# Moving the decode states and the W_out sums to other units, and one more pair of output rows as seven products

## The chip, the cores and the metric

The kernel runs on one core of a Trainium2 chip. The metric is device time in microseconds (us) of one execution of the whole program. Before the change three runs took 1107.13, 1110.31 and 1109.86 us, a median of 1109.86 us. One more execution was recorded by the profiler; it took 1107.08 us, and all views of the trace are views of it. TensorE (PE in the profile) does the matmuls, VectorE (DVE) and ScalarE (ACT) the elementwise work, GpSimd (POOL) small statistics; DMAs are issued by SyncE (SP), by ACT and by POOL, each with an in-order queue of its own.

## The reference

One layer of a hybrid decoder on 2048 prompt tokens and, beside them, one new token for each of 8 sequences ("decode"). Cut to what matters:

```python
h = rmsnorm(x, norm_g)
rq, rk, rv, rg, hq, hf, hi, hgate = split(h @ w_in, 8)          # 8 groups of 512 columns
o_ret, s_ret = recurrence(rotary(rq), rotary(rk) * dk**-0.5, rv, log_gamma, s_ret)   # 4 heads of 128
o_hg,  s_hg  = recurrence(silu(hq), (1 - lb) * sigmoid(-hf), hi, logf, s_hg)         # 4 heads of 128
o_cat = concat(head_rmsnorm(o_ret) * silu(rg), head_rmsnorm(o_hg) * silu(hgate))
y = rmsnorm(x + o_cat @ w_out, final_norm_g)
# recurrence: S_t = diag(f_t) S_{t-1} + k_t v_t^T ; o_t = S_t^T q_t
```

For the prompt the state starts at zero and the recurrence is computed in chunks. For the decode tokens it is one step from a given state: eight heads (four of retention, four of HGRN2), each with 8 states of 128x128. Outputs are y for both, and all new states. Every float32 operand is split into a high and a low part, and a product is three matmuls (high by high, high by low, low by high).

## The kernel before, in words

**Stages.** First the values (rv and hi) of all 2048 tokens are computed and put in DRAM (lines pv and pvd of the profile). Then come 16 *units*, numbered 0 to 15, two for each head and half of the sequence (`order`). Even units project an HGRN2 head, odd units a retention head. A unit's projection is three weight blocks of 128 columns (`sub_steps`, `seg_steps`, matmuls at L557). While a unit projects, the scan of the unit before it is merged in between its steps (`merge`): so an even unit carries a **retention** scan (`ret_rec`) and an odd unit an **HGRN2** scan (`hgrn_rec`), which has many more VectorE operations. Units 0 to 7 are the first half of the tokens, 8 to 15 the second. Units 0, 7, 8 and 15 run segment by segment with all three weights live (`SEG_MAJOR`). Scan results go to DRAM (`o_dram`).

**Side work.** `side_at` lists operations with a place, unit number plus fraction; `side_steps` and `place` put them among the projection steps. Before the change these are, all in units 8 to 15:

- the eight decode heads. `d_load` loads the 8 states S (512 KB) and the values, broadcast over partitions, vb (512 KB) on SP's queue. `d_state` multiplies vb by k (L937), for HGRN2 also S by f (L940); `d_add` adds them (L946, L948), copies the high part (ACT, L950) and writes the new state out on ACT's queue; `d_lo` makes the low part (L958); `d_mm` is two matmuls for each of two halves (L965), a copy and a write to `d_dram`.
- four `t_spool(k)`. Each loads two blocks of W_out (512 KB each), makes four differences of them (L906 to L909), splits two 128x1024 results into high and low (`split`, L106 and L107) and writes four parts of 512 KB to `t_dram` on ACT's queue. They are the sums T1 to T4 of W_out that the seven-product form needs.
- `d_norm`, `d_sq`, `d_ms`, `d_rs`, `d_tr`: reading the eight decode outputs back from `d_dram`, their head norm, and eight transposes on PE.

**Output stage.** 2048 rows are 16 chunks of 128. `PLAIN = 6` chunks are done directly (`out_steps`, 48 matmuls of 128x128x512 each, py in the profile); the first two are merged with the scan of unit 15, and there too lies `d_project`, the output projection of the decode tokens (32 matmuls, pyd). The other ten chunks go in pairs: `o_pair` computes a pair with seven products of four blocks (84 matmuls, po) after sums on the left (`op_s12`, `op_s34`) and with T1 to T4 on the right, read back from `t_dram` by `t_load` on POOL's queue, 1 MB for each high or low part. T4 is put in columns of `wo[0]` that the direct chunks read before.

**Buffers.** `rawp` has six slots of 4 KB a partition, used by loads of weights (wr), states and values (dS, dv), their high and low parts (ds), W_out (wot, wor), outputs (or), y rows and more. `wp` has three slots each for high and low weight parts (w_h, w_l), and `split` takes its results from there too. A slot is free when its last reader is done, a DMA out of it included.

**What sets the order.** PE's instructions run in the order in which the program text emits them. For the other engines and queues a planner orders the instructions beforehand: it walks the program with estimated durations and lets an engine take a later instruction when the earlier ones are not ready in its estimate and a buffer slot is free. On the chip each queue then runs strictly in that order, so an instruction that waits holds all behind it on its queue.

Of the kernel before, what the change touches and what calls it, by code (L numbers as in the profile page):

```python
# [10 lines left out]
F32 = mybir.dt.float32  # L11
F32R = mybir.dt.float32r
# [6 lines left out]
P = 128  # L19
# [22 lines left out]
def step_kernel(ctx, tc, a, out):  # L42
# [66 lines left out]
    def split(r, name):  # L109
        h = wp.tile([P, D], F32R, tag="wh", name=name + "h")  # L110
        l = wp.tile([P, D], F32R, tag="wl", name=name + "l")
        hi_lo(h, l, r)
        return h, l
# [785 lines left out]
        (x, n): dr.tile([P, 2, 4, GW], F32, tag=f"t{x}{n}", name=f"t_dram{x}{n}") for x in "hl" for n in range(2)  # L899
    }  # L900

    def t_spool(k):
        ra, rb, t = (rawp.tile([P, 2, GW], F32, tag="raw", name=f"wot{k}{n}") for n in range(3))
        for n, r in enumerate((ra, rb)):
            sp.dma_start(r.rearrange("p a b -> p (a b)"), a["w_out"][(k + 4 * n) * P : (k + 4 * n + 1) * P, :])
        dve.tensor_tensor(t[:, 1], rb[:, 1], ra[:, 1], op=ALU.subtract)  # L906
        dve.tensor_tensor(ra[:, 1], ra[:, 1], ra[:, 0], op=ALU.subtract)
        dve.tensor_tensor(t[:, 0], rb[:, 1], ra[:, 1], op=ALU.subtract)
        dve.tensor_tensor(ra[:, 0], t[:, 0], rb[:, 0], op=ALU.subtract)  # L909
        for n, src in enumerate((t, ra)):  # L910
            for x, y in zip("hl", split(src.rearrange("p a b -> p (a b)"), f"wos{k}{n}")):
                act.dma_start(t_dram[x, n][:, :, k], y.bitcast(F32).rearrange("p (a b) -> p a b", a=2))

    dec = {}

    def d_split(src, name):
        t = up.tile([P, 8, 40], F32R, tag="dhl", name=name, bufs=2)
        act.activation(t[:, :, 0:8], src, AF.Copy)
        act.activation(t[:, :, 8:32], zero.unsqueeze(1).to_broadcast([P, 8, 24]), AF.Copy)
        dve.tensor_tensor(t[:, :, 32:40], src, t[:, :, 0:8].bitcast(F32), op=ALU.subtract)  # L920
        return t
# [6 lines left out]
        sp.dma_start(vb, vd_dram[ty, :, h * P : (h + 1) * P].partition_broadcast(P))  # L928
        dec["l", hd] = (S, vb)

    def d_state(hd):
        ty, h = divmod(hd, NH)
        if hd == 0:
            dec["q"] = d_split(dq, "dq_hl")
        S, vb = dec["l", hd]
        kd = dk[:, hd].unsqueeze(2).to_broadcast([P, NB, P])
        dve.tensor_tensor(vb, vb, kd, op=ALU.mult)  # L937
        if ty == 1:
            fd = df[:, hd].unsqueeze(2).to_broadcast([P, NB, P])
            dve.tensor_tensor(S, S, fd, op=ALU.mult)  # L940

    def d_add(hd):
        ty, h = divmod(hd, NH)
        S, vb = dec["l", hd]
        if ty == 0:
            dve.scalar_tensor_tensor(S, S, GAMMA[h], vb, op0=ALU.mult, op1=ALU.add)  # L946
        else:
            dve.tensor_tensor(S, S, vb, op=ALU.add)  # L948
        sh, sl = (rawp.tile([P, NB, P], F32R, tag="raw", name=f"ds{t}{hd}") for t in "hl")
        act.activation(sh, S, AF.Copy)  # L950
        act.dma_start(
            out[("new_ret_sample", "new_hgrn_sample")[ty]][0, :, h].rearrange("b d v -> d b v"), S
        )
        dec["s", hd] = (sh, sl)

    def d_lo(hd):
        sh, sl = dec["s", hd]
        dve.tensor_tensor(sl, dec["l", hd][0], sh.bitcast(F32), op=ALU.subtract)  # L958

    def d_mm(hd, part):  # L960
        for i in (part,):
# [44 lines left out]
    def d_project():  # L1006
        ps = [ps_o.tile([40, 512], F32, tag="o", name=f"pyd{i}") for i in range(2)]
        t = rawp.tile([NB, 2, 512], F32, tag="raw", name="ydl")
        for i in range(2):
            m = 0  # L1010
            for k in range(KT):
                for w in wo[k // 4]:
                    pe.matmul(
                        ps[i], dec["od"][:, k], w[:, k % 4, i * 512 : (i + 1) * 512],
                        start=(m == 0), stop=(m == 2 * KT - 1),
                    )
# [280 lines left out]
    def o_pair(i, after):  # L1297
        ca, cb = 2 * i, 2 * i + 1
        last = cb == T // P - 1
        box = {}  # L1300
        lo, hi = slice(0, GW), slice(GW, D)
        ms = {c: sm.tile([P, 2], F32, tag="yms", name=f"yms{c}") for c in (ca, cb)}

        def keep(key, tag):
            box[key] = op.tile([P, GW], F32, tag=tag, name=f"o{key}_{i}")
            return box[key]

        for n, (x, w) in enumerate(PRODUCTS):
            ps = bank([P, GW], f"po{i}{n}")
            for k in range(4):  # L1310
                kk = slice(k * P, (k + 1) * P)
                three(ps, [t[:, kk] for t in oop[i, x]], [t[:, k] for t in Top[w]], k == 0, k == 3)
            xa, xb = xro[ca], xro[cb]
            if n == 0:
                act.activation(keep("s1", "t41"), ps, AF.Copy)
                dve.tensor_tensor(xa[:, lo], xa[:, lo], box["s1"], op=ALU.add)
            elif n == 1:
                dve.tensor_tensor(xa[:, lo], ps, xa[:, lo], op=ALU.add)
                y_sq(ca, lo, ms[ca][:, 0:1])
            elif n == 2:  # L1320
                dve.tensor_tensor(keep("u2", "t42"), ps, box["s1"], op=ALU.add)
                dve.tensor_tensor(xa[:, hi], xa[:, hi], box["u2"], op=ALU.add)
            elif n == 3:
                dve.tensor_tensor(keep("u3", "t43"), ps, box["u2"], op=ALU.add)
                dve.tensor_tensor(xb[:, hi], xb[:, hi], box["u3"], op=ALU.add)
                dve.tensor_tensor(xb[:, lo], xb[:, lo], box["u3"], op=ALU.add)
            elif n == 4:
                dve.tensor_tensor(xb[:, hi], ps, xb[:, hi], op=ALU.add)
                dve.tensor_tensor(xa[:, hi], ps, xa[:, hi], op=ALU.add)
                y_sq(cb, hi, ms[cb][:, 0:1])  # L1330
            elif n == 5:
                dve.tensor_tensor(xa[:, hi], ps, xa[:, hi], op=ALU.add)
                y_sq(ca, hi, ms[ca][:, 1:2])
                if not last:
                    y_out(ca, ms[ca], False)
            else:
                dve.tensor_tensor(xb[:, lo], xb[:, lo], ps, op=ALU.subtract)
# [4 lines left out]
            for f in after.get(n, ()):  # L1342
                f()

    p0 = PLAIN // 2
# [112 lines left out]
```

## Time and profile before

| what | value |
|---|---|
| median of three runs | 1109.86 us |
| profiled execution, whole / span of its instructions | 1107.08 us / 1105.3 us |
| PE, DVE, ACT, POOL busy | 97%, 66%, 36%, 11% of the span |
| mean granted TensorE clock | 0.989 of full speed |
| units 0 to 7 / 8 to 15 | 177.4 to 525.4 us / 525.4 to 919.4 us |
| last scan with two direct chunks and pyd | 919.4 to 957.9 us |
| four more direct chunks / five pairs / end | to 1001.4 / to 1096.7 / to 1105.3 us |

A profile row of stretches gives, for each stretch of time, each engine's busy us with the number of instructions, the granted clock (PEclk, 1.00 is full speed), the busy share of the DMA engines and the rate. The chain of waits follows the work that ended last back in time: start, duration, and what ran or was awaited. A wait row names the waiting engine and line, then what it waited for, then us in total, times, and the longest. Units begin where the first projection matmul of their first weight block starts.

### The profile page before, as it was taken

To read this page: it belongs to the slowest core of one execution; us is meant where nothing else is said; L and a number is where in the kernel's file an instruction comes from. 1 tells how busy PE (TensorE), PEld (TensorE's weight loads), DVE (VectorE), ACT (ScalarE), POOL (GpSimd) and SP (SyncE) were. 2 spreads that over 40 slices of the span, in tenths; PEclk is the share of its full clock that TensorE was granted. 3 is DMA by queue.
4 is the path that set the end of the run, shared out by engine and by line. 5 is a ranking of instruction groups with operands and counts; after the bars stand their busy time and mean duration, and the time that the engine had idled before them with its cause. 6 is when DMAs were issued, how large, how long until landed. Compare 5 with 4: busy or idle time off the path is not lost.

```text
span 1105.3 us, 21769 instructions
## 1 busy us (share of the span) xinstructions
PE 1071.9 (97%) x9042; PEld 915.3 (83%) x9042; DVE 734.5 (66%) x1262; ACT 403.1 (36%) x869; POOL 126.9 (11%) x218
## 2 busy tenths in 40 slices
PE   9999999999999999999999988998899899999996
PEld 7778888999999989989877877886688688788885
DVE  8676975574484485578767667747754776447874
ACT  7763332233233232325434342423332244322431
POOL 1310000001101101001010110101011102311211
PEclk9999999999999999999999998999899999999999
DMA  8564357212212212124633465346330243497432
GB/s 302 195 213 151 121 170 259 69 40 65 74 37 77 67 51 77 35 83 122 203 122 90 141 214 172 122 134 202 114 123 22 104 137 118 147 361 216 136 132 96
DMA packets 103588, 146.76 MB, mean 133 GB/s; under 512 B 5889, under 2 KB 69505, under 8 KB 102721
## 3 DMA queue, kind: packets, MB, share of 16 engines
q1 hardware_dynamic: 82880, 106.20, 30.5%
q0 software_dynamic: 6848, 24.74, 6.1%
q10 hardware_dynamic: 13760, 14.42, 3.8%
q8 instruction: 71, 1.16, 0.4%
q14 instruction: 29, 0.23, 0.1%
HBM read 105.70 MB, written 39.65 MB: 132 GB/s over the span
## 4 chain that ended last, share of the span: by engine, by line
PE 85%; DVE 6%; DMA 5%; issue 2%; ACT 1%; POOL 0%; DVEq 0%; POOLq 0%; ACTq 0%; SPq 0%
PE pjg L557 15%; PE pv L292 14%; PE po L292 8%; PE pjfh L557 8%; PE pjkr L557 7%; PE pjqh L557 6%; PE py L1184 6%; PE pjqr L557 5%; DMA dv<-vd_dram 2%; PE puh L669 1%; PE par L728 1%; PE poh L684 1%; PE poh L686 1%; PE plh L813 1%; PE pur L669 1%
## 5 line engine op out<-in xcount | busy, mean ns | idle before, releaser
L557 PE MATMUL pjg<-xh,w_l 128*128 128x512 f32 (+2 forms) x320 | 112.1, 350 | 4.8 <-DVE w_l L107 4.8
L557 PE MATMUL pjg<-xh,w_h 128*128 128x512 f32 (+2 forms) x320 | 116.2, 363 | 0.0
L557 PE MATMUL pjg<-xl,w_h 128*128 128x512 f32 (+2 forms) x320 | 111.3, 348 | 0.0
L106 ACT ACTIVATE w_h<-wr 128x1024 fp32r<-128x1024 f32 x48 | 50.6, 1058 | 72.8 <-PE pjg L557 31.0
L107 DVE TENSOR_TENSOR w_l<-wr,w_h 128x1024 fp32r<-128x1024 f32 x48 | 58.6, 1221 | 21.1 <-ACT w_h L106 14.3
L557 PEld LDWEIGHTS pjg<-xh,w_l 128*128 128x128 f32 x320 | 60.5, 189 | 13.2 <-DVE w_l L107 5.2
L557 PEld LDWEIGHTS pjg<-xh,w_h 128*128 128x128 f32 x320 | 60.7, 190 | 6.9
L557 PEld LDWEIGHTS pjg<-xl,w_h 128*128 128x128 f32 x320 | 60.7, 190 | 6.3
L793 ACT ACTIVATE kepth<-kh 128x1024 f32<-128x1024 f32 x24 | 25.5, 1062 | 104.2 <-DVE kh L783 104.2
L557 PE MATMUL pjkr<-xh,w_h 128*128 128x512 f32 (+2 forms) x160 | 59.7, 373 | 0.0
L557 PE MATMUL pjfh<-xh,w_h 128*128 128x512 f32 (+2 forms) x160 | 58.6, 366 | 0.0
L557 PE MATMUL pjqr<-xh,w_h 128*128 128x512 f32 (+2 forms) x160 | 58.3, 364 | 0.0
L557 PE MATMUL pjqh<-xh,w_h 128*128 128x512 f32 (+2 forms) x160 | 57.3, 358 | 0.0
L557 PE MATMUL pjkr<-xl,w_h 128*128 128x512 f32 (+2 forms) x160 | 57.2, 357 | 0.0
L557 PE MATMUL pjkr<-xh,w_l 128*128 128x512 f32 (+2 forms) x160 | 57.1, 357 | 0.0
L557 PE MATMUL pjfh<-xh,w_l 128*128 128x512 f32 (+2 forms) x160 | 55.7, 348 | 0.0
L557 PE MATMUL pjqh<-xh,w_l 128*128 128x512 f32 (+2 forms) x160 | 55.6, 348 | 0.0
L557 PE MATMUL pjqr<-xh,w_l 128*128 128x512 f32 (+2 forms) x160 | 55.6, 347 | 0.0
L557 PE MATMUL pjfh<-xl,w_h 128*128 128x512 f32 (+2 forms) x160 | 55.5, 347 | 0.0
L557 PE MATMUL pjqr<-xl,w_h 128*128 128x512 f32 (+2 forms) x160 | 55.5, 347 | 0.0
L557 PE MATMUL pjqh<-xl,w_h 128*128 128x512 f32 (+2 forms) x160 | 55.5, 347 | 0.0
L591 ACT ACTIVATE sg<-pjg 128x512 f32<-128x512 f32 (+2 forms) x40 | 20.3, 507 | 62.1 <-PE pjg L557 62.1
(773 smaller groups left out, 2898.0 us busy)
## 6 DMA issues: line engine op xcount, KB each, us to landing
wr<-in_w_in SPq DMA_DIRECT2D x48, 512.0 KB
xn<-in_x_prompt SPq DMA_DIRECT2D x32, 256.0 KB
v_dram<-vo SPq DMA_DIRECT2D x32, 256.0 KB
v<-v_dram SPq DMA_DIRECT2D x16, 512.0 KB
or<-o_dram SPq DMA_DIRECT2D x16, 512.0 KB
xr<-in_x_t SPq DMA_DIRECT2D x12, 512.0 KB
xr<-in_x_t SPq DMA_DIRECT2D x24, 256.0 KB
xro<-in_x_prompt SPq DMA_DIRECT2D x10, 512.0 KB
```

The lines of the kernel that those rows point to most:

```text
L106: act.activation(h, src, AF.Copy)
L107: dve.tensor_tensor(l, src, h.bitcast(F32), op=ALU.subtract)
L292: pe.matmul(ps, xx, ww, start=(first and n == 0), stop=(last and n == 2))
L557: pe.matmul(ps, ww[:, kk], x[:, k, b0 : b0 + n], start=(k == 0 and i == 0), stop=(k == KT - 1 and i == 2),)
L591: act.activation(sg[:, :n], ps, AF.Sigmoid)
L669: pe.matmul(pu[:, j], ksb[g][:, j], vcol(4 * g + j), start=True, stop=True)
L684: pe.matmul(po[:, j], A[:, c], vcol(c), start=True, stop=src is None)
L686: pe.matmul(po[:, j], qcol(c), src, start=False, stop=True)
L728: pe.matmul(pa[:, j], k[:, cc], q[:, cc], start=True, stop=True)
L793: act.activation(ss[:, 512:], k[:, :HALF], AF.Copy)
L813: pe.matmul(dst[32 * i : 32 * i + 32, c], kk, qq, start=True, stop=True)
L1184: pe.matmul(ps, o[:, kk], w[:, k % 4, i * 512 : (i + 1) * 512], start=(k == 0 and n == 0), stop=(k == KT - 1 and n == 2),)
```

## The change

1. The decode heads are placed at 8.45, 10.02, 10.48, 12.02, 12.33, 12.63, 14.02 and 14.45: all begin in even units. Before: 8.45, 9.05, 9.55, 10.2, 11.05, 12.1, 13.05, 14.2. Their steps are placed one by one: load at 0, the products at 0.12 and 0.17, the sum at 0.22, the high and low parts and the state's write at 0.27, the matmuls at 0.45 and 0.51.
2. `t_spool` becomes `t_load_raw`, four `t_sum` and two `t_spool`, each placed singly, from 0.5, 2.1, 4.1 and 6.1 on: units 0, 2, 4 and 6.
3. `d_norm` to `d_tr` move from units 14 and 15 to the first two direct chunks (after unit 15); `d_project` moves from there to the next direct chunks.
4. `PLAIN` goes from 6 to 4, so six pairs are done as seven products instead of five. The T loads and the first pair's left sums are spread over two direct chunks in place of four.
5. The seven products run in the order A11, A12, S2, S1, S4, S3, A22 (T3 and T4 last); in the last pair the first chunk's output is finished after the fifth product and written by POOL's queue, not after the last one.

```diff
-    def t_spool(k):
...
+    def t_load_raw(k):
+        traw[k] = [rawp.tile([P, 2, GW], F32, tag="raw", name=f"wot{k}{n}") for n in range(3)]
...
+    def t_spool(k, n):
+        ra, rb, t = traw[k]
+        for x, y in zip("hl", split((t, ra)[n].rearrange("p a b -> p (a b)"), f"wos{k}{n}")):
+            act.dma_start(t_dram[x, n][:, :, k], y.bitcast(F32).rearrange("p (a b) -> p a b", a=2))
...
-        t = up.tile([P, 8, 40], F32R, tag="dhl", name=name, bufs=2)
+        pl, tag = (up, "dhl") if name == "dq_hl" else (rawp, "raw")
+        t = pl.tile([P, 8, 40], F32R, tag=tag, name=name)
...
-    for hd, at in enumerate((8.45, 9.05, 9.55, 10.2, 11.05, 12.1, 13.05, 14.2)):
-        for n, f in enumerate((d_load, d_state, d_add, d_lo)):
-            side_at.append((at + (0, 0.18, 0.28, 0.38)[n], lambda f=f, hd=hd: f(hd)))
-        for n in range(2):
-            side_at.append((at + 0.55 + 0.07 * n, lambda hd=hd, n=n: d_mm(hd, n)))
-    side_at += [(at, lambda k=k: t_spool(k)) for k, at in enumerate((10.7, 11.5, 12.6, 13.5))]
-    side_at += [(14.95, d_norm), (15.15, d_sq), (15.22, d_ms), (15.4, d_rs), (15.5, d_tr)]
+    for hd, at in enumerate((8.45, 10.02, 10.48, 12.02, 12.33, 12.63, 14.02, 14.45)):
+        steps = [d_load, lambda hd: d_mul(hd, 0), lambda hd: d_mul(hd, 1), d_add, d_lo,
+                 lambda hd: d_mm(hd, 0), lambda hd: d_mm(hd, 1)]
+        for f, d in zip(steps, (0, 0.12, 0.17, 0.22, 0.27, 0.45, 0.51)):
+            side_at.append((at + d, lambda f=f, hd=hd: f(hd)))
+    for k, at in enumerate((0.5, 2.1, 4.1, 6.1)):
+        steps = [t_load_raw] + [lambda k, n=n: t_sum(k, n) for n in range(4)]
+        steps += [lambda k, n=n: t_spool(k, n) for n in range(2)]
+        for f, d in zip(steps, (0, 0.2, 0.23, 0.26, 0.29, 0.34, 0.44)):
+            side_at.append((at + d, lambda f=f, k=k: f(k)))
...
-    PLAIN = 6
+    PLAIN = 4
...
-    merge(fill, rec[:10] + [(3.5, d_project)] + rec[10:], 0.95)
+    fill = place(fill, [(0.05, d_norm), (0.3, d_sq), (0.4, d_ms), (0.55, d_rs), (0.7, d_tr),
+                        (0.75, lambda: dec.update(y=y_load(a["x_sample"], NB, "d")))])
+    merge(fill, rec, 0.95)
...
-        for n, (x, w) in enumerate(PRODUCTS):
+        for step, n in enumerate((0, 1, 2, 4, 5, 3, 6)):
+            x, w = PRODUCTS[n]
...
-                if last:
-                    y_out(ca, ms[ca], last)
                 y_out(cb, ms[cb], last)
...
+        (0.02, lambda: op_load(p0)), (0.02, lambda: t_load("T2", (0, 0))), (0.3, lambda: t_load("T1", (1, 1))),
+        (0.36, lambda: t_load("T3", (0, 1))), (0.42, d_project),
+        (0.3, lambda: op_s12(p0)), (0.4, lambda: op_s34(p0)), (0.5, lambda: op_a(p0)),
+        (0.6, lambda: xr_load(p0)), (0.7, lambda: op_s23(p0)), (0.8, lambda: op_s14(p0)),
+        (0.88, lambda: t_load("T4", (1, 0))), (0.9, lambda: op_a22(p0)),
```

More of the change, by code (lines that the diff above doesn't have):

```diff
@@ L900, in step_kernel, with t_sum @@
     }
-    def t_spool(k):
[L903 to L912, printed above, removed]
+    traw = {}
+    def t_load_raw(k):
+        traw[k] = [rawp.tile([P, 2, GW], F32, tag="raw", name=f"wot{k}{n}") for n in range(3)]
+        for n in range(2):
+            sp.dma_start(
+                traw[k][n].rearrange("p a b -> p (a b)"), a["w_out"][(k + 4 * n) * P : (k + 4 * n + 1) * P, :]
+            )
+    def t_sum(k, n):
+        ra, rb, t = traw[k]
+        if n == 0:
+            dve.tensor_tensor(t[:, 1], rb[:, 1], ra[:, 1], op=ALU.subtract)
+        elif n == 1:
+            dve.tensor_tensor(ra[:, 1], ra[:, 1], ra[:, 0], op=ALU.subtract)
+        elif n == 2:
+            dve.tensor_tensor(t[:, 0], rb[:, 1], ra[:, 1], op=ALU.subtract)
+        else:
+            dve.tensor_tensor(ra[:, 0], t[:, 0], rb[:, 0], op=ALU.subtract)
+    def t_spool(k, n):
+        ra, rb, t = traw[k]
+        for x, y in zip("hl", split((t, ra)[n].rearrange("p a b -> p (a b)"), f"wos{k}{n}")):
+            act.dma_start(t_dram[x, n][:, :, k], y.bitcast(F32).rearrange("p (a b) -> p a b", a=2))
     dec = {}
     def d_split(src, name):
-        t = up.tile([P, 8, 40], F32R, tag="dhl", name=name, bufs=2)
+        pl, tag = (up, "dhl") if name == "dq_hl" else (rawp, "raw")
+        t = pl.tile([P, 8, 40], F32R, tag=tag, name=name)
         act.activation(t[:, :, 0:8], src, AF.Copy)
@@ L929, in d_load, with d_mul @@
         dec["l", hd] = (S, vb)
-    def d_state(hd):
+    def d_mul(hd, n):
         ty, h = divmod(hd, NH)
-        if hd == 0:
-            dec["q"] = d_split(dq, "dq_hl")
         S, vb = dec["l", hd]
-        kd = dk[:, hd].unsqueeze(2).to_broadcast([P, NB, P])
-        dve.tensor_tensor(vb, vb, kd, op=ALU.mult)
-        if ty == 1:
+        if n == 0:
+            kd = dk[:, hd].unsqueeze(2).to_broadcast([P, NB, P])
+            dve.tensor_tensor(vb, vb, kd, op=ALU.mult)
+        elif ty == 1:
             fd = df[:, hd].unsqueeze(2).to_broadcast([P, NB, P])
@@ L948, in d_add, with d_lo @@
             dve.tensor_tensor(S, S, vb, op=ALU.add)
+        if hd == 0:
+            dec["q"] = d_split(dq, "dq_hl")
+    def d_lo(hd):
+        ty, h = divmod(hd, NH)
+        S, vb = dec["l", hd]
         sh, sl = (rawp.tile([P, NB, P], F32R, tag="raw", name=f"ds{t}{hd}") for t in "hl")
@@ L953, in d_add @@
         )
+        dve.tensor_tensor(sl, S, sh.bitcast(F32), op=ALU.subtract)
         dec["s", hd] = (sh, sl)
[L956 to L958 removed]
     def d_mm(hd, part):
@@ L1321, in o_pair @@
                 dve.tensor_tensor(keep("u2", "t42"), ps, box["s1"], op=ALU.add)
[L1322 to L1326, printed above, removed]
             elif n == 4:
-                dve.tensor_tensor(xb[:, hi], ps, xb[:, hi], op=ALU.add)
-                dve.tensor_tensor(xa[:, hi], ps, xa[:, hi], op=ALU.add)
-                y_sq(cb, hi, ms[cb][:, 0:1])
+                dve.tensor_tensor(keep("u4", "t43"), ps, box["u2"], op=ALU.add)
+                dve.tensor_tensor(xa[:, hi], xa[:, hi], box["u4"], op=ALU.add)
+                dve.tensor_tensor(xb[:, hi], xb[:, hi], box["u4"], op=ALU.add)
             elif n == 5:
@@ L1333, in o_pair @@
                 y_sq(ca, hi, ms[ca][:, 1:2])
-                if not last:
-                    y_out(ca, ms[ca], False)
+                y_out(ca, ms[ca], False)
+                dve.tensor_tensor(xb[:, lo], xb[:, lo], box["u2"], op=ALU.add)
+            elif n == 3:
+                dve.tensor_tensor(xb[:, hi], ps, xb[:, hi], op=ALU.add)
+                dve.tensor_tensor(xb[:, lo], ps, xb[:, lo], op=ALU.add)
+                y_sq(cb, hi, ms[cb][:, 0:1])
             else:
@@ L1338, in o_pair @@
                 y_sq(cb, lo, ms[cb][:, 1:2])
-                if last:
-                    y_out(ca, ms[ca], last)
                 y_out(cb, ms[cb], last)
-            for f in after.get(n, ()):
+            for f in after.get(step, ()):
                 f()
```

6 lines of the change are left out of this document (1 added, 5 removed).

## The prediction

> **What bounds the kernel now.** I read the page's busy times first, then the rows of stretches cut at the unit borders, then the chain of waits in the second half, then the wait lists.
>
> ```profile
> PE 1071.9 (97%) x9042; PEld 915.3 (83%) x9042; DVE 734.5 (66%) x1262; ACT 403.1 (36%) x869; POOL 126.9 (11%) x218
> ```
>
> ```profile
> 346.70:389.10 42.40, 42.40 (x298) 39.39 (x296) 19.18 (x43) 12.07 (x34) 3.83 (x7) 1.00 0.22 70
> 389.10:435.70 46.60, 46.60 (x711) 42.45 (x710) 34.43 (x67) 16.19 (x38) 3.40 (x6) 1.00 0.17 52
> ...
> 525.40:567.60 42.20, 42.20 (x228) 35.91 (x226) 30.70 (x50) 17.50 (x36) 4.42 (x7) 1.00 0.56 174
> 567.60:620.10 52.50, 48.33 (x648) 39.62 (x646) 37.81 (x60) 19.75 (x43) 3.63 (x7) 1.00 0.38 114
> 620.10:666.90 46.80, 44.02 (x234) 36.52 (x233) 29.31 (x50) 15.96 (x37) 6.28 (x8) 1.00 0.57 178
> 666.90:720.60 53.70, 49.94 (x646) 41.35 (x645) 40.94 (x65) 20.17 (x42) 4.41 (x7) 0.94 0.49 152
> 720.60:767.50 46.90, 43.33 (x232) 36.11 (x230) 26.75 (x46) 15.14 (x35) 4.90 (x8) 1.00 0.47 151
> 767.50:821.70 54.20, 50.31 (x648) 41.55 (x645) 38.59 (x61) 20.35 (x42) 3.61 (x7) 0.94 0.43 132
> 821.70:864.50 42.80, 42.80 (x231) 36.24 (x229) 17.25 (x35) 11.45 (x31) 5.21 (x9) 1.00 0.22 74
> 864.50:919.40 54.90, 50.06 (x651) 41.13 (x650) 41.83 (x66) 21.56 (x43) 8.34 (x11) 0.94 0.31 104
> ...
> 957.90:1001.40 43.50, 43.50 (x193) 36.02 (x193) 22.54 (x28) 10.40 (x21) 11.96 (x25) 1.00 0.87 308
> 1001.40:1096.70 95.30, 95.23 (x421) 78.54 (x419) 69.30 (x93) 30.86 (x62) 17.68 (x40) 1.00 0.42 141
> ```
>
> PE is the bound: in units 4 and 5 (first two stretches) it is busy all the time, as it is in the output stage (last two). The exception is the second half, units 8 to 15, the eight rows between. Unit 8 (42.2 us) and unit 14 (42.8) have no idle PE; the six others have 2.8 to 4.8 us each (length less PE busy), 23.0 us in sum, and three of them run at a clock of 0.94.
>
> What is lost is more than the idle time, so I count it against an undisturbed unit. A head's matmuls are two pairs like this one from the chain of waits, 0.93 us:
>
> ```profile
> 600.11 0.47 PE pd L965 x2
> ```
>
> An even unit, undisturbed: unit 8, 42.2, and unit 14 less its head's matmuls, 42.8 - 0.93, on average 42.0. An odd one: 4.2 more, as unit 5 against unit 4, so 46.2. Units 8 to 15 last 919.4 - 525.4 = 394.0 us. Undisturbed they would last 4 x (42.0 + 46.2) + 8 heads x 0.93 + 0.6 for the eight decode transposes = 360.8. **The second half loses 33.2 us**: 4.4 in unit 9, 2.9 in 10, 6.6 in 11, 4.0 in 12, 7.1 in 13, 8.1 in 15.
>
> To what? The longest pieces of the chain of waits there are DMAs:
>
> ```profile
> 637.53 6.34 DMA dv<-vd_dram
> 647.91 5.96 DMA t_draml<-wos01l
> 669.04 8.72 DMA dS<-in_state_hgrn
> 682.31 6.58 DMA t_draml<-wos11l
> 696.04 4.32 PE pjkr L557 x18
> 737.16 7.96 DMA dv<-vd_dram
> 769.63 8.38 DMA t_draml<-wos30l
> ```
>
> VectorE stands in its queue until a state has landed, or until a spooled sum has been written and its slot in `wp` is free; the evictions that PE needs stand behind it. The loads come late because the six slots of `rawp` are taken, by a spool (first row below, SP's queue) or by a state still being written (second); a late weight then stops PE directly (third).
>
> ```profile
> SPq L928 <- DVE wos20l L107: 13.9, 1, 13.9
> ```
>
> ```profile
> SPq L130 <- DMA out_new_ret_sample<-dS: 16.4, 2, 9.2
> ```
>
> ```profile
> PE pjg L557 <- DVE w_l L107: 4.8, 1, 4.8
> ```
>
> **The change, part by part.** *(a) Spools leave the second half.* Units 10 to 13 have spools, unit 15 the read-back of (c); units 8 and 14, which lose nothing, have neither. One spool's work, by these two groups: four differences of 0.69 and two low parts of 1.23, 5.2 us of VectorE.
>
> ```profile
> L906 DVE TENSOR_TENSOR wot<-wot,wot 128x512 f32<-128x512 f32 x4 | 2.8, 692 | 7.0 <-DMA wot<-in_w_out 7.0
> ```
>
> ```profile
> L107 DVE TENSOR_TENSOR wos20l<-wot,wos20h 128x1024 fp32r<-128x1024 f32 x1 | 1.2, 1227 | 1.0 <-ACT wos20h L106 1.0
> ```
>
> In units 0, 2, 4, 6 this lies under PE: unit 4 has 19.2 of 42.4 us of VectorE taken, 24.4 with a spool; without that cover it would cost its 5.2. Its two loads go on SP's queue, ahead only of weights and values; its writes, 16 of 512 KB in all, on ACT's queue where DMA is 0.22 busy. What can show is the second split's wait for the first one's write (8.4 us above, with 0.1 unit, 4.2 us, between them): 4 us of standing VectorE and ACT. A spool costs from 0 to 3.45 (the mean of units 10 and 12, all blamed on it). I stay near the lower end, as the host units have no state work: 0.5 each, **+2.0**; both ends, 0 to +13.8.
>
> *(b) Heads begin in even units.*
>
> ```profile
> L937 DVE TENSOR_TENSOR dv<-dv,dk 128x1024 f32<-128x1024 f32 x8 | 9.8, 1226 | 17.3 <-DMA dv<-vd_dram 12.9 <-issue 4.4
> ```
>
> A head costs VectorE three operations of 1.23 (four for HGRN2), 3.7 to 4.9 us; unit 12, with one and two of them, gets 13.5 us on top of the 17.25 of 42.8 of unit 14. Capacity is there. But a place binds only PE: the planner pulls the rest forward. Head 3, its products placed at 10.38, ran in unit 9, which ends at 620.1:
>
> ```profile
> 608.36 1.23 DVE L937 TENSOR_TENSOR dv<-dv,dk 128x1024 f32<-128x1024 f32 x1 [2.17 <-DMA dv<-vd_dram]
> ```
>
> So some heads will still be worked on in odd units. A head cost nothing in unit 8, and 4.4 / 2 = 2.2 in unit 9, which had two and no spool. For seven heads (the first stays where it was) that is 0 to 15.4. The spools' slots are free, but the high and low parts of two heads (four slots) wait for their place on PE, so I take the middle: **+8**.
>
> *(c) The read-back* leaves unit 15, whose 8.1 us are in the 33.2 and hold this wait:
>
> ```profile
> 859.02 4.22 DMA d_dram<-de
> ```
>
> In the direct chunks the writes that it reads are a unit old, and the transposes on PE are placed 0.15 of the stage after their operand's last operation. Cost 0 to 4.2 (the same wait again); near 0, because nothing young is read: **+0.5**. `d_project` moves its 7.4 us of PE (below) from one stage to the next, nothing in the sum.
>
> *(d) Six pairs.* 96 matmuls become 84.
>
> ```profile
> 937.60 7.41 PE pyd L1013 x32
> ```
>
> ```profile
> 1001.43 92.49 PE po L292 x408
> ```
>
> 92.49 / 408 = 0.227 us, 12 x 0.227 = **-2.7**, all on PE's path. The new product order has as many VectorE operations a pair as the old one, and they fill 69.3 of 95.3 us.
>
> *(e) The end.*
>
> ```profile
> 1096.24 0.39 PE L292 MATMUL po<-woh,op7A22l 128*128 128x512 f32 x1
> ```
>
> ```profile
> 1093.95 0.69 DVE L1332 TENSOR_TENSOR xro<-po,xro 128x512 f32<-128x512 f32 x1 [1.43 <-PE po L292]
> 1096.70 1.42 DVE L1292 SCALAR_TENSOR_TENSOR xro<-xro,yms,rst 128x512 f32<-128x512 f32 x2 [2.06 <-POOL yms L103]
> 1098.03 0.68 DVE L1337 TENSOR_TENSOR xro<-xro,po 128x512 f32<-128x512 f32 x1
> ```
>
> The last matmul ends at 1096.6, but its subtraction starts at 1098.03, behind the other chunk's two scalings. The sixth product's addition started as its matmuls ended (1093.95), so the last one could start at 1096.7: **-1.4**. That chunk's write goes earlier, on POOL's queue, with only its partner's three short statistics behind it.
>
> **Sum:** -33.2 + 8 + 2 + 0.5 - 2.7 - 1.4 = -26.8. The profiled execution, 1107.1 us (span 1105.3), becomes 1080.3. The median of the runs shown is 2.8 above it, so I expect 1083.
>
> Of the 33.2, about 0.06 x (53.7 + 54.2 + 54.9) = 9.8 are clock. The Trainium skill, page "TensorE: Matmul & The Clock Gate", section "What's actually happening", says that the clock falls to half after an idle window of about 3.4 us; the trace agrees in part, for unit 9's 4.2 us idle, in pieces, ran at 1.00. By that rule head waits that stay short cost no clock, as I count; long ones would double the 8 and give 1091.
>
> **The rivals.** *Half stays.* The planner puts all seven heads in odd units (15.4) and each spool costs half of what it did (6.9): -33.2 + 15.4 + 6.9 + 0.5 - 4.1 = -14.5, as a median 1095.4. For it: head 3 above. Against it: units 11, 13 and 15, which lose most, have spools or the read-back.
>
> *T comes late.*
>
> ```profile
> 967.10:994.80 27.70, 27.70 (x124) 22.95 (x123) 12.43 (x15) 7.65 (x15) 5.42 (x11) 1.00 0.93 361
> ```
>
> ```profile
> oT3h<-t_dramh POOLq DMA_DIRECT2D x1, 1024.0 KB, 16.4
> ```
>
> ```profile
> woh<-t_dramh POOLq DMA_DIRECT2D x1, 1024.0 KB, 6.1
> ```
>
> Eight loads of 1 MB now have two direct chunks (96 x 0.227) and `d_project`, 29.2 us, plus the products before each is used (for T4 six of 2.72, so 45.5 us in). At 361 GB/s they take 23.2 us, so bandwidth suffices. But T4 overwrites columns of `wo[0]` and is placed after 15 of 16 steps, 27.9 us in; if one part lands in 16.4 and the other 6.1 after it, that is 50.4, and PE waits 4.9: 1088. The Trainium skill, "DMA: Bandwidth & Descriptors", section "Measured", gives 6.15 us for 1 MB; eight in a row would be 49.2, an estimate, and that speaks against this change too, by 3.7 us; the 361 GB/s measured with several in flight speaks for no wait.
>
> *Slots held until a write lands (slower).* Unit 12 takes three heads through six slots. If each waits for the slot of the one before, a head is a chain of load 8.7, VectorE 3.7, some 0.4 to issue and write 9.2, 22 us: 66 against 42 in unit 12, 44 in units 10 and 14, 28 us late; and if weights behind these loads on SP's queue stop PE for 4.8 us once in each of the three units, 14.4 more. Together 42.4, against 33.2 + 4.1 = 37.3 that can be saved: 1112.2, as a median 1115. From 40.6 us on it makes the kernel measurably slower. For it: SP's wait of 9.2. Against it: units 9, 11 and 13 leave slots to load ahead.
>
> *It does not do what it says.* The order is planned anew everywhere and the waits move rather than go: 33 again, (d) and (e) are eaten by the spools' 2 to 4: 1109.
>
> **How the numbers follow.** Forecast 0.58, half stays 0.22, T late 0.12, waits only moved 0.04, slower 0.04. The likeliest alone spans 1073 (heads, spools and read-back at nothing, -37.3) to 1091. The range for 8 in 10 goes on to the half-stays case and some 3 us above it: 1072 to 1099. 0.3%, 3.3 us, is about what a measurement can tell from no change here. The first three cases are faster by more: 0.92; same 0.04; slower 0.04.
>
> **What would show it.** (a): no `wos` in the second half, and PE idle below 0.5 us in each of units 0 to 6. (b): units 9, 11, 13 of 46 to 49 us at clock 1.00, and VectorE's wait for dv, 17.3 us, below 8. (c): unit 15 near 47 us. (d): 504 po matmuls that start without a wait on T. (e): the last subtraction within 0.2 us of the last matmul. The prediction is wrong if units 8 to 15 still take over 385 us, if SP's waits for state writes grow and units 10 or 12 pass 50 us, or if the first half or the pairs show idle PE of more than 5 us.

## The result: 1082 us, and where the profile after lost and kept its time

The changed kernel takes a median of 1082.09 us over four runs (1080.79 to 1084.99), against 1110.09 us for the kernel before: a ratio of 0.9755, 95% interval 0.9726 to 0.9784. Its profiled execution took 1081.12 us, with a span of 1079.3 us, 26.0 us less than the span of before.

First the page's busy times of the changed kernel. PE has 12 matmuls fewer and is still the bound.

```profile
PE 1061.1 (98%) x9030; PEld 908.3 (84%) x9030; DVE 742.4 (69%) x1274; ACT 407.3 (38%) x872; POOL 125.8 (12%) x219
```

Then its stretches, columns as before: unit 1, then units 8 to 15, then the direct chunks and the six pairs (to 1071.6; the end, to 1079.3, is 7.7 us).

```profile
211.30:258.90 47.60, 46.97 (x712) 42.66 (x711) 37.88 (x78) 18.77 (x40) 2.80 (x5) 1.00 0.35 119
...
526.60:569.30 42.70, 42.70 (x229) 36.16 (x228) 27.60 (x46) 16.90 (x36) 4.35 (x7) 1.00 0.54 157
569.30:620.40 51.10, 46.81 (x640) 38.84 (x639) 38.30 (x60) 18.34 (x40) 3.55 (x7) 1.00 0.34 96
620.40:664.20 43.80, 43.80 (x235) 36.86 (x234) 20.91 (x39) 13.52 (x34) 4.89 (x8) 1.00 0.35 102
664.20:711.00 46.80, 46.55 (x642) 38.82 (x640) 37.96 (x60) 18.54 (x39) 3.65 (x7) 1.00 0.36 96
711.00:754.70 43.70, 43.70 (x235) 36.70 (x233) 22.11 (x40) 14.57 (x35) 4.80 (x8) 1.00 0.41 124
754.70:804.20 49.50, 47.41 (x648) 39.25 (x646) 40.02 (x62) 19.41 (x41) 3.63 (x7) 1.00 0.35 107
804.20:848.00 43.80, 43.80 (x235) 36.81 (x234) 18.66 (x37) 13.71 (x33) 4.81 (x8) 1.00 0.26 86
848.00:896.20 48.20, 46.57 (x642) 38.57 (x640) 40.03 (x62) 21.71 (x44) 8.22 (x11) 1.00 0.32 99
```

```profile
896.20:957.20 61.00, 61.00 (x315) 49.05 (x313) 31.32 (x46) 19.35 (x47) 14.33 (x27) 1.00 0.65 232
957.20:1071.60 114.40, 114.40 (x505) 94.41 (x503) 90.74 (x120) 38.34 (x76) 23.22 (x54) 1.00 0.48 158
```

The kernel before, over the same last stages (six direct chunks with `d_project`, five pairs; its end, to 1105.3, is 8.7 us):

```profile
919.40:1001.40 82.00, 82.00 (x401) 66.30 (x400) 44.37 (x59) 25.66 (x58) 19.73 (x40) 1.00 0.65 223
1001.40:1096.60 95.20, 95.20 (x421) 78.54 (x419) 69.30 (x92) 30.86 (x62) 17.61 (x40) 1.00 0.42 141
```

The 26.0 us come from three places. The border to the output stage is the first matmul of py, at 896.2 here and at 919.1 in the kernel before; the 919.4 given for it above lies 0.3 too late. By this border units 8 to 15 take 896.2 - 526.6 = 369.6 us in place of 919.1 - 525.4 = 393.7: -24.1. The first half takes 349.0 in place of 348.0, all of the difference in unit 1, and begins 0.3 later. The output stage takes 183.1 in place of 186.2: -3.1. All even units of the second half now run with PE busy to the end, and units 11 and 15 nearly so (0.3 and 1.6 us idle). Units 9 and 13 do not, and no unit of this execution lost any clock.

What VectorE waited longest for at a DMA in units 8 to 15 of the changed kernel (line, what it waited for, us in total, times, longest), and pieces of the chain of waits around the border of units 8 and 9:

```profile
DVE dv L950 <- DMA dv<-vd_dram: 10.0, 4, 4.6
```

```profile
563.08 1.24 DVE w_l L107
...
564.33 6.30 DMA dv<-vd_dram
...
573.18 4.14 DMA out_new_ret_sample<-dS
...
577.39 5.91 DMA dv<-vd_dram
```

A product of a head still stands in VectorE's queue before its values have landed. The load takes about 6 us from its issue. It is also issued late: by the chain, the first of these loads was released by the low part of a weight, the second by the write of the first head's state, which lasted 4.14 us.

### The profile page after: what moved, and what is told of

Its sections match the earlier page's. It is cut to its first block, busy times and chain, and to the rows that moved or that the text cites. A ratio compares the mean times of both kernels' runs of the same rounds, so it can differ in the third digit from the quotient of the medians.

```text
span 1079.3 us, 21758 instructions
## 1 busy us (share of the span) xinstructions
PE 1061.1 (98%) x9030; PEld 908.3 (84%) x9030; DVE 742.4 (69%) x1274; ACT 407.3 (38%) x872; POOL 125.8 (12%) x219
## 4 chain that ended last, share of the span: by engine, by line
PE 89%; DVE 6%; DMA 3%; issue 1%; POOL 1%; ACT 1%; DVEq 0%; POOLq 0%; ACTq 0%; SPq 0%
PE pv L292 15%; PE pjg L557 14%; PE po L292 11%; PE pjfh L557 8%; PE pjqh L557 8%; PE pjkr L557 7%; PE pjqr L557 5%; PE py L1203 4%; DMA dv<-vd_dram 2%; PE pur L669 1%; PE puh L669 1%; PE par L728 1%; PE por L684 1%; PE poh L684 1%; PE poh L686 1%; PE por L686 1%
```

## The experiments

All ratios are to the kernel before, measured beside it on the same chip. Its median there was 1110.2 to 1112.8 us, and all its profile rows come from an execution of 1107.1 us; so the ratios can show several us more than the stretches do.

**The spools alone.** The kernel before, with `t_spool` in single steps at 0.5, 2.1, 4.1 and 6.1.

```diff
-    side_at += [(at, lambda k=k: t_spool(k)) for k, at in enumerate((10.7, 11.5, 12.6, 13.5))]
+    for k, at in enumerate((0.5, 2.1, 4.1, 6.1)):
+        steps = [t_load_raw] + [lambda k, n=n: t_sum(k, n) for n in range(4)]
+        steps += [lambda k, n=n: t_spool(k, n) for n in range(2)]
...
```

> The kernel before with the four W_out spools alone moved to units 0, 2, 4 and 6, singly placed. Theory (the loss of the second half comes from operations on VectorE's queue that wait for DMAs, the spools and the read-back first): units 10 to 13 lost 20.6 us and keep only what heads cost, about 2 us each; unit 15 still loses its 8. Units 8 to 15 about 378 us (394.0 before), first half +1, in all 13 to 17 us faster than before, ratio near 0.987. Rival (what counts is that heads are placed in units with a retention scan): the heads are where they were, so at most 5 us faster, ratio 0.995 or above.

Measured: 1093.43 us, 0.9832 [0.9811, 0.9854]. Its stretches of units 8, 13 and 15:

```profile
526.40:568.60 42.20, 42.20 (x227) 35.98 (x226) 30.80 (x50) 17.36 (x36) 4.47 (x7) 1.00 0.57 174
...
759.80:807.50 47.70, 47.36 (x645) 39.38 (x644) 34.89 (x57) 18.21 (x40) 3.54 (x7) 1.00 0.23 67
...
850.30:904.90 54.60, 49.04 (x651) 40.32 (x650) 41.83 (x65) 21.26 (x43) 8.20 (x11) 0.94 0.32 105
```

The second half lasts 904.9 - 526.4 = 378.5 us: the spools are worth 15.2 of the 24.1, inside the expected 13 to 17 (by the medians it is 19.4). Unit 13 has lost its disturbance; unit 15, with the read-back, has kept all of it.

**The heads' places alone.** The kernel before, its spools where they were, with the new places and single steps of the heads; the read-back from 15.05 on.

```diff
-    for hd, at in enumerate((8.45, 9.05, 9.55, 10.2, 11.05, 12.1, 13.05, 14.2)):
+    for hd, at in enumerate((8.45, 10.02, 10.48, 12.02, 12.33, 12.63, 14.02, 14.45)):
```

> The kernel before with the heads' new places and single steps alone; spools stay in units 10 to 13, and the read-back begins at 15.05, since the last head's matmuls now lie at 14.96. Theory (a place binds PE only, the spools still hold slots): within 5 us of before to either side, ratio 0.995 to 1.005; the spool writes stay in the chain of waits. Rival (places count): 12 us or more faster, ratio 0.989 or below.

Measured: 1103.7 us, 0.9926 [0.9902, 0.9951], between the two expectations. The second half takes 391.6 us, 2.1 less than before, but unevenly: unit 13, with spool and heads in it, is worse than before.

```profile
761.40:819.80 58.40, 50.92 (x646) 41.83 (x645) 45.38 (x69) 22.18 (x44) 4.46 (x7) 0.94 0.53 169
```

**The read-back put back.** The changed kernel with `d_norm` to `d_tr` in unit 15.

```diff
+    side_at += [(15.05, d_norm), (15.25, d_sq), (15.32, d_ms), (15.5, d_rs), (15.6, d_tr)]
...
-    fill = place(fill, [(0.05, d_norm), (0.3, d_sq), (0.4, d_ms), (0.55, d_rs), (0.7, d_tr),
-                        (0.75, lambda: dec.update(y=y_load(a["x_sample"], NB, "d")))])
+    fill = place(fill, [(0.75, lambda: dec.update(y=y_load(a["x_sample"], NB, "d")))])
```

> The changed kernel with the read-back, norm and transposes of the decode outputs put back into unit 15 (from 15.05 on), all else as changed. Theory: the read-back makes VectorE wait in unit 15 for young writes and adds five operations of about 1.2 us to the VectorE queue of an HGRN2 scan: unit 15 goes from 48.2 to 52 to 56 us, 4 to 8 us slower than the changed kernel. Rival (unit 15 lost time for another reason, its W_out loads): within 1 us of the changed kernel.

Measured: 1090.65 us, 0.98 [0.9773, 0.9828]. Unit 15 of this kernel, and what PE waited for in it:

```profile
851.80:908.50 56.70, 50.01 (x648) 41.03 (x647) 42.02 (x65) 23.99 (x48) 8.14 (x11) 0.94 0.32 102
```

```profile
PE pjkr L557 <- DVE w_l L107: 4.7, 1, 4.7
```

By the ratios this costs 5 us, within the 4 to 8 expected. Unit 15 is 8.5 us longer (56.7 against 48.2): 4.7 are this stop of PE, which waits for the low part of a weight, 3.4 the clock behind it (0.94 of the stretch) and 0.6 the transposes. VectorE waits for no DMA in it, though the chain of waits still runs through the write of the decode outputs (2.9 us) and their reading back (2.3) ahead of the first operation on them. The kernel before shows the same wait in its unit 15 (4.8 us for `w_l`). There three operations of the read-back, 3.6 us, and a wait of 1.2 us for its data stand ahead of that low part, and VectorE works without a pause in between.

But it is not the work itself that left unit 15 with the change. The four operations of the read-back on VectorE (`do`, 1.2 us each) still run in unit 15 of the changed kernel, drawn forward by the planner; only they stand behind the splits of the weights. The last low part of a weight there, and the first and the last of the four:

```profile
848.33 1.22 DVE L107 TENSOR_TENSOR w_l<-wr,w_h 128x1024 fp32r<-128x1024 f32 x1
...
881.15 1.20 DVE L1001 TENSOR_TENSOR do<-do,do 8x1024 f32<-8x1024 f32 x1
...
892.29 1.21 DVE L1012 TENSOR_TENSOR do<-do,dms 8x1024 f32<-8x1024 f32 x1
```

With the read-back put back:

```profile
861.03 1.21 DVE L1001 TENSOR_TENSOR do<-do,do 8x1024 f32<-8x1024 f32 x1
...
862.78 1.20 DVE L107 TENSOR_TENSOR w_l<-wr,w_h 128x1024 fp32r<-128x1024 f32 x1
```

So the read-back costs its place in the planned order, rather than the long DMA wait that I had quoted. In this last run only one of its operations stands ahead of the late low part, and ScalarE too made the high parts late (from 857.1 us on; the last one of the changed kernel at 847.0). Why the planner put the splits so late there is not shown.

**Heads placed in odd units.** The changed kernel with seven of the heads one unit earlier.

```diff
-    for hd, at in enumerate((8.45, 10.02, 10.48, 12.02, 12.33, 12.63, 14.02, 14.45)):
+    for hd, at in enumerate((8.45, 9.02, 9.48, 11.02, 11.33, 11.63, 13.02, 13.45)):
```

> The changed kernel with seven heads placed one unit earlier, in units with an HGRN2 scan: 9.02, 9.48, 11.02, 11.33, 11.63, 13.02, 13.45; all else as changed. Theory (the planner pulls the work forward by half a unit or more whatever the place, and waits come from late loads): within 4 us of the changed kernel to either side. Rival (units with a retention scan are what makes the heads cheap): each of the seven costs 2 us more, 10 us or more slower than the changed kernel.

Measured: 1078.61 us, 0.97 [0.968, 0.9721]: not slower but a little faster than the changed kernel, by the ratios 5 to 6 us, more than the 4 that the expectation allowed. That the places lie in units with a retention scan is not what helps. VectorE even waits longer for values than in the changed kernel:

```profile
DVE dv L950 <- DMA dv<-vd_dram: 17.8, 7, 4.1
```

So the total of these waits is not their price either. Of the heads' 28 operations on VectorE, counted by their start in the timeline, 14 ran in odd units in the kernel before, 19 in the changed kernel and 8 in this one. The place binds the matmuls; the planner draws the rest forward by about a unit, so places in odd units put the work into even ones, and the other way round.

**Two more sets of places**, with the changed kernel beside them on the same chip.

> The changed kernel itself, once more, beside the next three. By both theories the ratio that it had, 0.9755, within 0.003. In its planned order 14 of VectorE's 21 head operations of units 9 to 13 and later (products, sums, low parts) stand in units 9, 11 and 13.

```diff
+    for hd, at in enumerate((8.45, 9.45, 10.0, 11.45, 11.8, 12.2, 13.45, 13.9)):
```

> The changed kernel with the heads placed at 8.45, 9.45, 10.0, 11.45, 11.8, 12.2, 13.45, 13.9: five of eight begin in units with an HGRN2 scan or at their end. In the planned order 8 head operations stand in units 9, 11 and 13, against 14. Theory (the planned place on VectorE counts, not the place in the list): units 9, 11 and 13 together 4 to 8 us shorter than in the changed kernel, the whole 3 to 7 us faster than it. Rival (the place in the list counts): 5 us or more slower than it.

```diff
+    for hd, at in enumerate((8.45, 10.4, 10.7, 12.4, 12.6, 12.8, 14.2, 14.45)):
```

> The changed kernel with the heads placed later in the same even units: 8.45, 10.4, 10.7, 12.4, 12.6, 12.8, 14.2, 14.45; every head still begins in a unit with a retention scan. In the planned order 20 head operations stand in units 9, 11 and 13, against 14. Theory (the planned place on VectorE counts): these units together 4 to 9 us longer, the whole 4 to 9 us slower than the changed kernel. Rival (the place in the list counts): within 2 us of it.

Measured: the changed kernel 1083.03 us, 0.9746 [0.9724, 0.9769]; the first set (9 of the 28 operations ran in odd units) 1083.54 us, 0.9756 [0.9734, 0.9779]; the second (22 of them) 1089.31 us, 0.9806 [0.9781, 0.983]. The second came out as expected. The first did not: fewer operations in odd units brought nothing, since VectorE stood for values in unit 9 at a moment at which PE then waited in a single piece, and the clock fell. Unit 9 of the first set, and PE's wait in it:

```profile
569.30:623.00 53.70, 48.99 (x646) 40.83 (x645) 35.17 (x59) 18.54 (x40) 4.13 (x7) 0.94 0.29 94
```

```profile
PE plh L813 <- DVE qth L786: 4.7, 1, 4.7
```

**A slot of their own for the values.** Then vb would be loaded ahead, I thought, whatever `rawp` holds.

```diff
-    vp = rctx.enter_context(tc.tile_pool(name="vp", bufs=3))
+    vp = rctx.enter_context(tc.tile_pool(name="vp", bufs=2))
+    dp = rctx.enter_context(tc.tile_pool(name="dp", bufs=1))
...
-        vb = rawp.tile([P, NB, P], F32, tag="raw", name=f"dv{hd}")
+        vb = dp.tile([P, NB, P], F32, tag="vb", name=f"dv{hd}")
```

> The changed kernel with the broadcast values vb in one buffer slot of their own instead of one of rawp's six (paid with the third slot of the scan's values). Places as changed. Theory (loads land late because rawp's slots are taken): VectorE's wait for dv falls from 10 us to below 4, unit 9 from 51.1 to 47 to 48 us, the whole 2 to 5 us faster than the changed kernel. Rival (the loads are late because the transfer itself takes 6 to 9 us): the wait stays, within 1.5 us of the changed kernel.

Measured: 1095.0 us, 0.986 [0.9836, 0.9885], some 12 us slower than the changed kernel. Both expectations fall, but the edit does not test the theory as I meant it to. With one slot SP holds each load until the sum of the head before is done (second row, and 18.7 us more for the retention heads), and VectorE waits more, not less:

```profile
DVE dv L951 <- DMA dv<-vd_dram: 15.8, 6, 3.6
```

```profile
SPq L943 <- DVE dS L962: 19.6, 3, 8.0
```

The slot was also paid for with the third slot of the scan's values, and what that cost is not separated. Whether slots of `rawp` make the loads late thus stays open here; the chain of the changed kernel speaks for it.

**No loads.** Is it the wait for a load, or the heads' work itself, that units 9 and 13 pay for? Heads 1 to 7 read data that are in SBUF anyway; their part of the decode output is left out.

```diff
-        sp.dma_start(S, (a["state_ret"], a["state_hgrn"])[ty][0, :, h].rearrange("b d v -> d b v"))
-        sp.dma_start(vb, vd_dram[ty, :, h * P : (h + 1) * P].partition_broadcast(P))
+        if hd == 0:
+            sp.dma_start(S, (a["state_ret"], a["state_hgrn"])[ty][0, :, h].rearrange("b d v -> d b v"))
+            sp.dma_start(vb, vd_dram[ty, :, h * P : (h + 1) * P].partition_broadcast(P))
...
+            dve.tensor_tensor(vb, held(0) if hd else vb, kd, op=ALU.mult)
```

> The changed kernel, but heads 1 to 7 load neither their states nor their values: the three or four VectorE operations of a head read 1024 columns of the input activations that are in SBUF anyway (this part of the decode output is left out). The planned VectorE order has the same head operations in units 9, 11 and 13 as before, and one more in unit 11. Theory (what units 9 and 13 lose is VectorE standing in its queue for a load, 5.4 us in unit 9 and 3.8 in unit 13): these waits are gone, unit 9 takes 46.4 to 47.5 in place of 51, unit 13 47 to 48 in place of 49.5 to 51, the even units stay at 43.8, the second half falls by 5 to 9 us and the time by as much, to a ratio of 0.967 to 0.971 where the changed kernel has 0.9755. Rival (the head's VectorE work itself overfills an odd unit): units 9 and 13 lose at most 1.5 us each, ratio 0.973 to 0.976.

Measured: 1080.83 us, 0.9727 [0.97, 0.9753], between the two expectations and next to the rival's. The units say more. Units 9, 11 and 13 of this kernel:

```profile
569.00:616.20 47.20, 46.26 (x642) 38.70 (x640) 36.48 (x59) 18.26 (x40) 3.61 (x7) 1.00 0.21 66
...
659.90:708.00 48.10, 46.35 (x642) 38.66 (x640) 38.34 (x61) 18.34 (x39) 3.58 (x7) 1.00 0.17 54
...
751.70:801.10 49.40, 47.41 (x648) 39.24 (x646) 39.16 (x61) 19.53 (x41) 3.62 (x7) 1.00 0.22 65
```

Unit 9 falls from 51.1 to 47.2, and one operation of 1.2 us less in it can't be all of that: there it was mostly the wait for the loads, or their traffic, which the edit takes away as well. Unit 13 stays at 49.4, with the same two stops of PE as in the changed kernel, though VectorE's wait of 3.8 us for a state is gone: there it is the work, or its place in the queue. Unit 11, with one operation more, rises from 46.8 to 48.1. Each theory holds in a unit of its own.

**All heads' work tied to even units.** Two heads in each of units 8, 10, 12 and 14. A small operation multiplies the first columns of k or q that this same unit projects by zero and adds the head's k or f; the products read its result, so no planner can draw them forward.

```diff
+    PIN = (("k", 0), ("k", 0), ("k", 0), ("q", 0), ("k", 0), ("q", 0), ("k", 0), ("q", 0))
...
+            for j, src in enumerate((k_, f_)[: 1 + ty]):
+                dve.scalar_tensor_tensor(
+                    dec["p", hd][:, j], cur["u"][key][:, c : c + NB], 0.0, src, op0=ALU.mult, op1=ALU.add
+                )
...
+    for hd, at in enumerate((8.3, 8.6, 10.02, 10.4, 12.02, 12.4, 14.02, 14.4)):
```

> The changed kernel, with two heads in each of units 8, 10, 12 and 14, and each head's products tied to the first columns of k or q that the same unit has projected (a small operation multiplies them by zero and adds the head's k or f), so that the planned VectorE order has no operation of a head in an odd unit. The loads and the work are the same. Theory (a wait costs only in an odd unit, whose VectorE has no slack; the place in the program does not hold the planner, a dependence does): units 9, 11 and 13 take 46.2 to 47, units 8 to 14 even 42.7 to 44.5, the second half 361 to 364 in place of 369.6 to 372, the ratio 0.967 to 0.971. Rival (the same waits arise wherever the work is, as the slots bind): two even units grow by 3 us or more and the ratio stays at 0.973 or above.

Measured: 1074.97 us, 0.9675 [0.9652, 0.9697], faster than the changed kernel. Its units 8, 11 and 12 (unit 13 is as unit 11):

```profile
526.20:572.80 46.60, 44.27 (x227) 36.97 (x226) 32.16 (x53) 17.40 (x37) 5.03 (x7) 0.96 0.55 174
...
663.80:710.10 46.30, 46.30 (x643) 38.73 (x642) 31.78 (x54) 16.18 (x37) 3.57 (x7) 1.00 0.16 50
710.10:753.90 43.80, 43.80 (x236) 36.77 (x234) 27.86 (x48) 15.69 (x36) 5.62 (x8) 1.00 0.49 149
```

Units 11 and 13 have no idle PE left, with VectorE at 31.8 of 46.3 us in place of 38 to 40. Unit 12 takes two HGRN2 heads, 27.9 us of VectorE, for nothing. Only unit 8 lost 3.9 us: a product stood there 4.0 us for its values, amid the loads of the next inputs, PE stopped for 2.3 us, and the clock fell to 0.96. So a wait can cost in an even unit too.

**The same, with the first two heads untied in unit 8.**

```diff
+    PIN = (None, None, ("k", 0), ("q", 0), ("k", 0), ("q", 0), ("k", 0), ("q", 0))
...
+    for hd, at in enumerate((8.45, 9.02, 10.02, 10.4, 12.02, 12.4, 14.02, 14.4)):
```

> The kernel with all heads' work tied to even units, but heads 0 and 1 at 8.45 and 9.02 without the tie, so that in unit 8 the order is again the one of the changed kernel (two heads one after the other, which there cost nothing), in place of a product that stood 4.0 us for its values amid the loads of the next input block. Theory (the 3.8 us that unit 8 lost are that wait, in a unit that shares SP's queue with eight loads of inputs): unit 8 back to 42.7, unit 9 46.3 to 47.2, the others as they were, the second half 361 to 363 us and the ratio 0.963 to 0.966. Rival (unit 8 loses them to the work of two heads beside the splitting of the inputs, whatever their order): unit 8 45 us or more, the ratio 0.9665 to 0.969.

Measured: 1074.59 us, 0.9665 [0.9646, 0.9684]. Unit 8 is at 42.6 us again, as expected, but unit 9 grew from 47.2 to 48.5, which was not. The second half lasts 362.9 us, yet the ratio lies at the edge of the rival's range; between this version and the one before it there is no clear difference. Both beat the changed kernel by 0.7% to 0.9%.

**Six direct chunks again.**

```diff
-    PLAIN = 4
+    PLAIN = 6
```

> The changed kernel with six direct chunks and five pairs as before, all else as changed. Theory (d): 12 matmuls of 0.227 us more, the output stage 2.7 us longer (185.8 in place of 183.1 us), the ratio 0.0025 higher, 0.977 to 0.979. Rival (the sixth pair gives its matmuls back in waits for T or in VectorE work): output stage within 1 us of 183.1, ratio 0.974 to 0.9765.

Measured: 1095.8 us, 0.9863 [0.984, 0.9886]. Both expectations fall: the output stage is 13.2 us longer (196.3). The stretch of the third and fourth chunk, PE's wait, and the chain behind it:

```profile
957.00:980.00 23.00, 14.18 (x56) 11.30 (x55) 9.62 (x12) 7.24 (x16) 3.26 (x8) 0.85 0.71 245
```

```profile
PE py L1203 <- DVE yc L1161: 8.8, 1, 8.8
```

```profile
955.86 9.27 DMA out_y_prompt<-yc
...
965.20 3.73 DMA yc<-in_x_prompt
...
969.02 0.70 DVE yc L1161
```

The 12 matmuls are 2.7 of it. 8.8 are a wait: the input rows of a chunk need a slot of `rawp` that an output still being written holds, and PE waits for the bank that the addition has to empty. About 1.5 are the clock, 0.85 there (14.18 - 56 x 0.227). The new order of loads was written for four chunks, so this run does not price the sixth pair by itself.

## Why the prediction was right, point by point

The forecast was -26.8 us and 1083; measured were -26.0 in the profiled executions and a median of 1082.09. Faster by over 0.3% held.

| step | forecast, us | measured, us |
|---|---|---|
| second half, loss gone less heads (a, b) | -33.2 + 8 = -25.2 | -24.1 |
| spools in the first half (a) | +2.0 | +1.0 (and 0.3 of start) |
| read-back, pairs and end (c, d, e) | 0.5 - 2.7 - 1.4 = -3.6 | -3.1 |

*(a)* Right, and the largest part: 15.2 us by the spools alone. They cost 1.0 and not 2.0, and at another place than I said. Spools do wait for writes in units 2, 4 and 6, and weights for them (VectorE up to 3.5 us, ScalarE up to 3.4 at once), but PE does not idle there:

```profile
378.21 1.23 DVE L107 TENSOR_TENSOR w_l<-wr,w_h 128x1024 fp32r<-128x1024 f32 x1 [3.53 <-DMA t_draml<-wos21l]
```

All of the cost is in unit 1, which carries an HGRN2 scan. A low part of the first spool ran in it (at 212.7 us), ScalarE stood 1.9 us for that spool's write before it could split a weight, and at 233.4 PE idled 0.6 us for VectorE. The four sums of the second spool, placed from 2.3 on, ran in unit 1 too, but behind this stop (237.3 to 242.2). Which of the first two it was is not separated. "Below 0.5 in each of units 0 to 6" failed there by 0.1.

*(b)* The size was right, the reason half right. The heads cost 4.9 us in unit 9 (51.1 less 46.2), 0.6 in unit 11 and 2.4 in unit 13 (49.5 less 46.2 and 0.93 for a head's matmuls), 7.9 in sum against the 8 taken. The 8 was the middle of 0 to 15.4, so that it fits so well is luck. That "a place binds only PE" is shown by the seven heads placed in odd units, which ran no slower, and by the count: the changed kernel has more of the heads' work in odd units than the kernel before. But the forecast marks missed: units 9 and 13 passed 49, and VectorE's wait for dv was 10.0, not below 8 (of the 17.3 that I gave for before, 12.9 were this wait and 4.4 were not). The step that failed is the price put on "some heads will still be worked on in odd units": I took it for waits, and without loads unit 13 lost as much. Places were worth little once the spools were gone. From the run with spools alone to the one with the read-back put back, units 9 to 14 fell from 281.7 us to 281.3. In the changed kernel they take 278.7, but each of the other two executions lost some 3.4 us of clock in these units, and this one none.

*(c)* The 8.1 us of unit 15 went down to 2.0 (48.2 less 46.2). 1.8 are left too in the versions that have no head's work in units 13 and 15, and 1.6 of them are a stop of PE at the unit's end, for an eviction of the scan:

```profile
895.78 0.66 PE L699 MATMUL poth<-ident,obh 128*128 128x128 f32 x4 [1.57 <-DVE oth L701]
```

The mechanism was wrong in two points. "Leaves unit 15" did not happen on VectorE, whose four operations run there still; and "hold this wait" of 4.22 us was not what cost. VectorE stood 1.2 us for what it read back, and not at all with the read-back put back, where unit 15 lost no less. What the 8.1 us were is one late low part (4.8) and the clock behind it (3.4).

*(d)* Right. Direct chunks and pairs took 177.5 us (919.1 to 1096.6) and take 61.0 + 114.4 = 175.4, with PE busy all the time in both kernels; with the 0.6 of the transposes that moved there, 12 matmuls gave 2.1 + 0.6 = 2.7, as forecast. No matmul of a pair waited for T, so *T comes late* did not happen.

*(e)* The order came as forecast: in the timeline of the end the last subtraction starts as the last matmul (389 ns long) ends.

```profile
1071.23 0.39 PE L292 MATMUL po<-woh,op7A22l 128*128 128x512 f32 x1
```

```profile
1071.66 0.69 DVE L1358 TENSOR_TENSOR xro<-xro,po 128x512 f32<-128x512 f32 x1 [0.21 <-PE po L292]
```

From the last matmul to the end it is 7.7 us in place of 8.7: 1.0 of the 1.4, since the statistics and the write after it took 0.4 longer.

*The rivals.* *Half stays* (1095) is what the spools alone give, for another reason than I wrote: of the 8.9 us between the two second halves (378.5 and 369.6), 6.4 lie in unit 15, with the read-back. *Slots held* happened on a small scale, as the chain at the border of units 8 and 9 shows, but units 10 and 12, at 43.8 and 43.7 us, did not grow by it.

*The clock.* Three stretches of the kernel before ran at 0.94, 9.8 us by the forecast's estimate; in the changed kernel's execution none did. So some two fifths of the second half's gain are clock, and another execution of the same kernel lost some of it again (last section). The Trainium skill, "TensorE: Matmul & The Clock Gate", section "What's actually happening", gives an idle window of about 3.4 us, free-running. The trace agrees where the stop is one piece: 4.7 us in unit 9 of the first set of places, clock 0.94. It agrees less below that: see the last section.

## What to carry to other kernels

A shared queue is priced by the slack of the stage: much the same waits and work of VectorE were free beside the retention scan, but for one wait of 4.0 us in unit 8, and paid beside the HGRN2 scan, where VectorE was 75 to 81% busy. Where a planner may draw operations forward, a place in the program text does not hold them; a dependence on something that the right stage produces does. That was worth 0.7% to 0.9%. The new places gave 0.5% to 1.0% by the ratio beside the spools, though only 2.1 us by the stretches, and next to nothing without the spools. Before undoing one part of a change to price it, look at what was rearranged around it: six direct chunks among loads placed for four cost 13 us, of which 2.7 were theirs.

## What the hardware showed that I had not expected

The same stops of PE cost clock in one execution and none in another. Unit 13 of the changed kernel ran again on another chip, with PE idle for 2.0 us as before (2.1) and no stop over 1.1 us:

```profile
755.80:806.80 51.00, 48.96 (x648) 40.41 (x645) 40.00 (x62) 19.34 (x41) 3.63 (x7) 0.97 0.35 104
```

It took 51.0 us and not 49.5, all of it in slower matmuls (48.96 against 47.41 us busy). The clock does not sink a little for the whole unit: it stands at 0.50 for 3.4 us, which costs half of that, 1.7 us, and elsewhere for twice as long. In the kernel before these times begin at 684.4, 786.8, 882.4 and 1100.8 us. The distances are 30, 28 and 64 times 3.413 us, so they lie on a fixed grid, whose cells of 3.4 us take no notice of when PE stops. These are two cells of that grid around the two stops, in the execution that lost clock:

```profile
777.80:781.20 3.40, 1.45 (x45) 1.37 (x46) 3.37 (x6) 2.84 (x8) 0.00 (x0) 1.00 0.19 76
781.20:784.60 3.40, 3.40 (x14) 2.71 (x12) 3.19 (x5) 0.99 (x2) 0.00 (x0) 0.50 0.02 5
```

And in the execution that lost none:

```profile
774.80:778.20 3.40, 2.37 (x40) 1.72 (x39) 3.40 (x7) 1.72 (x3) 0.00 (x0) 1.00 0.44 154
778.20:781.60 3.40, 2.34 (x29) 2.01 (x22) 3.34 (x6) 2.86 (x7) 0.00 (x0) 1.00 0.00 0
```

In the first, both stops fall into one cell, and PE is busy for 1.45 of its 3.4 us; in the second, the border of two cells lies between them. All fourteen traces, laid out on their grids up to the last matmul, agree on what decides it: of the cells at full clock, each with PE busy for less than 1.5 us was followed by one at 0.50, and none with more than 1.8 us was; between the two, both occur. So it is not the length of a stop that counts but what is left of PE's work in its cell. The single stop of 2.3 us in unit 8 of the version tied to even units left 1.28 us (clock 0.96); the 4.3 us of idle in unit 9 of the changed kernel, in pieces of at most 1.2, left 2.0 in the worst cell (clock 1.00). Where the grid lies differs from one execution to the next, and so short stops bring a spread of 1.7 us, or 3.4, each time that one falls badly.
